# An SSM chunk scan on Trainium2: both channel groups kept on the partitions, signed phases in whole tiles on VectorE, output products of 64 rows

## The chip, the cores and the metric

The program runs on one core of a Trainium2 chip. A time is that of one execution on the device, in microseconds (us). The kernel before took 1131.76 us (median of three runs, 1124.91 to 1132.9). Where a profile is shown, it is one execution recorded by the hardware profiler. Engines are called PE (TensorE; PEld is its weight load), DVE (VectorE), ACT (ScalarE), POOL (GpSimd) and SP (SyncE, which here mostly issues DMAs).

## The reference, cut to what matters

A decoder trunk of two layers on 256 tokens, D = 1024, FF = 2816, all in fp32. Layer 0 has a SwiGLU FFN, differential attention, a second FFN and a gated embedding (ple); layer 1 the same with a diagonal state space model (SSM) and a gated linear unit (GLU) in place of attention. The change is in this SSM:

```python
def s5_glu(h, ...):          # 64 groups of 16 channels, 64 complex states each
    a_bar = jnp.exp(lam_dt); b_bar = ((a_bar - 1.0) / lam)[:, :, None] * b
    def chunk_step(state, u_c):                  # x[t] = a x[t-1] + b u[t], chunk by chunk
        bu = jnp.einsum('gph,bcgh->bcgp', b_bar, u_c.astype(jnp.complex64))
        _, xs = lax.associative_scan(combine, (a, bu), axis=1)
        xs = xs + a_pow[None] * state[:, None]
        y = jnp.einsum('ghp,bcgp->bcgh', c, xs).real + d_g * u_c
        return xs[:, -1], y
    ...
    z = jax.nn.gelu(y) @ w_glu + b_glu
    return z[..., :D_MODEL] * jax.nn.sigmoid(z[..., D_MODEL:])
```

## The kernel before, in words

**Threads and products.** The two blocks of 128 tokens (b = 0, 1) are two generators that share weight tiles, so their work alternates on every engine. Each large product is made of three fp32r products, hi x hi, lo x hi and hi x lo (`mm3`, L302 to L304). The order of instructions on each engine is fixed at build time by the Tile framework's scheduler, which plays the program through with its own estimates of durations and with priorities; on the chip each engine then runs its list strictly in that order.

**Weights** (`Weights`, L86 to L134) are streamed. SP issues a load of 512 KB into one of three `raw` buffers (L119), ACT casts it to `hi` (L131), VectorE makes `lo` = raw - hi (L133), and then the raw buffer is free for the next load. `hi` and `lo` come from pools of nine buffers each. The tiles of the GLU's weight `ssm_w_glu` have the numbers 252 to 267 (`raw252`, `hi252`, `lo252` and so on). Pairs of the same pools also take ready tables from DRAM (L111): for the SSM a `t_d` tile in `hi` and an `o_d` tile in `lo`.

**Tables** (`ssm_tables`, L754 to L965) are made while the FFN of layer 1 runs, about 330 to 680 us. They hold powers of a, the phases `er` and `ei` (cosine and sine of the rotation), the decay `rh`, and for each of 8 group packs (`gp`, eight groups) the complex products `vr`, `vi` and `or`, `oi` (`products`, L892 to L900, on POOL; `vr`/`vi` go through PE transposes `v_ps`, `or`/`oi` are stored to `o_d` by SP), and copies `cp` of C (L914, L915). POOL also computes the factors of the norms (`r_pre`, `r_pnple`, L313 to L317) for the layer's main work, between these. At the end POOL moves the Toeplitz blocks from `m_d` to `t_d` (L963).

**Scan stage** (`ssm_core`, L1005 to L1152, about 815 to 861 us). u is transposed to `ush`; `s_ps` = V u (chunks of 8 tokens) is copied to `ssmS` by ACT (L1076). Then, for each of four *pairs* `pr` (two group packs each, a tile 128x512 that holds real and imaginary part):
- PE transposes into `st_ps` (L1082), rows = 2 channel groups (e) x 64 states.
- VectorE rotates: t1 = st*er (L1101), t2 = swapped st*ei (L1110, L1111; for pairs 1 and 2 on POOL from a copy that ACT makes, L1104, L1106), w = t1 +- t2 (L1112 or L1107, L1108).
- two scans (L1114), one for the real and one for the imaginary part, turn w into y.
- it is rotated back: t1 = y*er (L1116 on VectorE), t2 on POOL (L1117, L1118).
- X, the state ahead of each chunk, is t1 +- t2 shifted by one, in four operations of 64 rows (L1125, L1126): the 64 rows of one e become two halves (real, imaginary) of a tile of 128 rows, in `ssmS` for even pairs, in `ush` for odd ones.
- PE accumulates `y_ps`: products(pr) = t_d * u (L1047) and outputs(pr) = o_d * X (L1058), each 16 products of 128 rows x 32 columns (each an instruction twice in the trace, since they are fp32). ACT applies gelu (L1065), one ACTIVATE of 128x512 for each pair.

The outputs of pair pr-1 are issued after X of pair pr. At the end the gelu's result is transposed (`y_tr`, L1146) and split into `yThi` (ACT, L325) and `yTlo` (VectorE, L326): half 0 comes from the pairs 0 and 1, half 1 from 2 and 3. The GLU (`zglu`, L302 to L304) begins with the products on half 0.

The line that turns a pair's products on its groups:

```python
nc.tensor.matmul(out_ap[32 * q:32 * q + 32], st_[:, 32 * q:32 * q + 32], w[:, q * P:(q + 1) * P], ...)   # grouped, q = 0..3
```

Of the kernel before, what the change touches and what calls it, by code (L numbers as in the profile page):

```python
# [9 lines left out]
F32 = mybir.dt.float32  # L10
F32R = mybir.dt.float32r
BF16 = mybir.dt.bfloat16
AF = mybir.ActivationFunctionType
ALU = mybir.AluOpType
AX = mybir.AxisListType

P = 128
# [23 lines left out]
 'pt2': [1, 2],  # L41
# [10 lines left out]
 'wait2': {},  # L52
 'xpr': [[1, 2, 3], []]}
# [89 lines left out]
def trunk(ctx, tc, x, p, norm_g, ffn_w_in, ffn_w_out, attn_w_qkv, attn_w_o, attn_lam, attn_subln_g,  # L143
          rel_bias, ssm_lam_re, ssm_lam_im, ssm_log_dt, ssm_b_re, ssm_b_im, ssm_c_re, ssm_c_im, ssm_d, ssm_w_glu,
          ssm_b_glu, ple_w_proj, ple_w_gate, out):
    nc = tc.nc
# [547 lines left out]
    ssm = {}  # L694
# [59 lines left out]
    def ssm_tables(pool, keep):  # L754
# [51 lines left out]
        ei = keep.tile([P, 8, 4, 32], F32, tag="ei", name="ei", bufs=1)  # L806
# [8 lines left out]
        ssm["er"], ssm["ei"], ssm["rh"] = er, ei, rh  # L815
# [12 lines left out]

# [37 lines left out]
        for nm, src in (("re", ssm_c_re), ("im", ssm_c_im)):  # L866
            ct = pool.tile([P, 4, 8, 16], F32, tag=f"c{nm}", name=f"c{nm}", bufs=1)
            csrc = src[0].rearrange("(a g) h p -> (g h) a p", g=8)
            for hf in range(2):
                cn = pool.tile([P, 4, 2, 64], F32, tag="cn", name=f"cn{nm}{hf}", bufs=1)  # L870
                for d_ in range(2):
                    nc.sync.dma_start(cn[:, :, d_, :], csrc[:, 4 * hf:4 * hf + 4, :])
                pt = bank("a1", f"c_ps{nm}{hf}")
                for a in range(4):
                    nc.tensor.transpose(pt[:, a * P:(a + 1) * P], cn[:, a].rearrange("p d n -> p (d n)"), ident)
                pv = pt.rearrange("p (q g e h) -> p q g e h", q=2, g=8, e=2)
                for e in range(2):
# [14 lines left out]
        def products(out_r, out_i, ar_, ai_, br_, bi_, nm):  # L892
# [4 lines left out]
            g.tensor_tensor(out_r, out_r, t, ALU.subtract)  # L897
# [8 lines left out]
        for gp in range(8):  # L906
# [34 lines left out]
            products(o_r, o_i, *A, *C, f"o{gp}")  # L941
# [58 lines left out]
    def take2(n):  # L1000
        W.advance(min(used[1] + NB, n + NB), n)
        used[0] = used[1] = n
        return W.tiles[n]

    def ssm_core(pool, vs, tos):  # L1005
# [28 lines left out]
        xfs = [[t[:, 2048 + 256 * e:2304 + 256 * e].rearrange("p (c j) -> p c j", j=32) for e in range(2)]  # L1034
               for t in (S_xf, ush_xf)]
# [5 lines left out]
        def grouped(out_ap, st_, w, **flags):  # L1041

            for q in range(4):
                nc.tensor.matmul(out_ap[32 * q:32 * q + 32], st_[:, 32 * q:32 * q + 32], w[:, q * P:(q + 1) * P],
                                 skip_group_check=True, **flags)

        def products(pr):  # L1047
            acc = ps_acc.tile([P, 512], F32, tag="acc", name=f"y_ps{pr}")
            nc.tensor.matmul(acc, zeros[:, :P], zeros, start=True, stop=False, skip_group_check=True)
            for gg in range(2):  # L1050
                tt, to = take2(tos[2 * pr + gg])
                for e in range(2):
                    j = 2 * gg + e
                    grouped(acc[:, j * P:(j + 1) * P], ush[:, 4 * pr + j, :], tt[:, e * 512:e * 512 + 512],
                            start=False, stop=False)
            return acc

        def outputs(pr, acc):  # L1058
            for gg in range(2):
                tt, to = W.tiles[tos[2 * pr + gg]]  # L1060
                for e in range(2):
                    j = 2 * gg + e
                    grouped(acc[:, j * P:(j + 1) * P], X[pr][e][:, gg * P:(gg + 1) * P], to[:, e * 512:e * 512 + 512],
                            start=False, stop=True)
            nc.scalar.activation(yg[:, pr // 2, :, 4 * (pr % 2):4 * (pr % 2) + 4, :].rearrange("p t g h -> p g t h"),  # L1065
                                 acc.rearrange("p (g t h) -> p g t h", g=4, t=8), AF.Gelu_apprx_tanh)

        for pr in range(4):
# [15 lines left out]
            er, ei, rh = (ssm[k][:, 2 * pr:2 * pr + 2].rearrange("p g q j -> p (g q j)") for k in ("er", "ei", "rh"))  # L1084
            er2 = er.rearrange("p (o x) -> p o x", o=1).broadcast_to([P, 2, 256])

            if pr % 2:
                r4 = big_pool.tile([P, 5, 2, 256], F32, tag="hT_lo1", name=f"rt{pr}")
                r4 = [r4[:, j] for j in range(5)]
            else:  # L1090
                r4 = [act_pool.tile([P, 2, 2, 256], F32, tag=f"xT_{x}{pr // 2}", name=f"rt{x}{pr}") for x in ("hi", "lo")]
                r4 = [t[:, j] for t in r4 for j in range(2)]

            def rt(nm):
                if nm == "s" and pr % 2 == 0:
                    return work.tile([P, 2, 256], F32, tag="sg", name=f"rts{pr}")
                return r4["abcds".index(nm)]
# [233 lines left out]
```

## Time and profile before

| | before |
|---|---|
| runs | 1131.76, 1124.91, 1132.9 us |
| profiled execution, its own time | 1130.13 us |
| its span (first to last instruction) | 1128.3 us |
| mean granted clock of PE | 0.971 |
| busy: PE, DVE, ACT, POOL | 1044.2, 694.4, 553.4, 258.9 us |
| moved by DMA | 218.62 MB |

The span is cut by time: what stands at 830 us of it happens in the scan stage. A row of a timeline has a start and a duration (a group of like instructions is put together in one row), then engine, line, operation, what it writes and what it reads; in brackets how long the engine had idled and who ended that. The granted clock is given as a part of full speed: 1.00 is 2.4 GHz, 0.50 is 1.2 GHz.

### The profile page before, as it was taken

The page shows a single profiled execution, that of the slowest core. Times are in us where ns is not written, and L with a number is a line of the kernel's source. Part 1 is how long each engine was busy: PE and PEld are TensorE (multiplying, and loading weights), DVE is VectorE, ACT ScalarE, POOL GpSimd, SP SyncE. Part 2 cuts the span into 40 slices and gives each one's busy share as a digit, 9 for nine tenths or more (in the row PEclk, how much of TensorE's full clock was granted, in tenths as well). Part 3 has the DMA queues.
Part 4 walks back from the last instruction along what each step waited for, and adds up shares of the span by engine and source line. Part 5 has one row for each costly group of instructions (what it writes and reads, how often), then busy time and mean ns, then how long its engine had stood idle before and what let it go on. Part 6 is the DMA issues. An engine that isn't in the chain of part 4 may idle for free. (4 is left out here: it accounts for less than half of the span.)

```text
span 1128.3 us, 14341 instructions
## 1 busy us (share of the span) xinstructions
PE 1044.2 (93%) x5123; PEld 836.1 (74%) x5123; DVE 694.4 (62%) x1011; ACT 553.4 (49%) x873; POOL 258.9 (23%) x315
## 2 busy tenths in 40 slices
PE   6899999999998999999787997999867999999997
PEld 4688888788776887777565886888645878888885
DVE  6555554679658896545568572654368675555464
ACT  5544443566665544443464542544244465444354
POOL 6000000000021007898879521000131010000001
PEclk9899999999999999999899998999987999999999
DMA  7766656567547767676555768756784557665651
GB/s 225 229 175 190 194 175 203 169 188 220 158 94 181 215 196 211 187 221 218 170 169 165 195 207 314 237 178 210 207 350 151 178 175 223 188 187 165 209 168 56
DMA packets 119815, 218.62 MB, mean 194 GB/s; under 512 B 25024, under 2 KB 43488, under 8 KB 119744
## 3 DMA queue, kind: packets, MB, share of 16 engines
q1 hardware_dynamic: 116864, 211.71, 61.3%
q0 software_dynamic: 1824, 5.33, 1.8%
q8 instruction: 40, 0.66, 0.2%
q10 hardware_dynamic: 1056, 0.66, 0.2%
q14 instruction: 31, 0.25, 0.1%
HBM read 205.13 MB, written 16.74 MB: 197 GB/s over the span
## 5 line engine op out<-in xcount | busy, mean ns | idle before, releaser
L133 DVE TENSOR_TENSOR lo<-raw,hi 128x1024 fp32r<-128x1024 f32 x332 | 427.5, 1294 | 271.1 <-ACT hi L131 269.4
L131 ACT CAST hi<-raw 128x1024 fp32r<-128x1024 f32 x332 | 347.6, 1051 | 334.7 <-PE up L304 105.5
L302 PE MATMUL up<-hi,xThi 128*128 128x512 f32 x704 | 279.6, 400 | 14.1 <-ACT hi L131 5.6
L304 PE MATMUL up<-hi,xTlo 128*128 128x512 f32 x704 | 280.3, 403 | 0.1
L303 PE MATMUL up<-lo,xThi 128*128 128x512 f32 x704 | 278.8, 397 | 1.6 <-DVE lo L133 1.6
L302 PEld LDWEIGHTS up<-hi,xThi 128*128 128x128 f32 x704 | 134.4, 191 | 43.5 <-ACT hi L131 6.4
L303 PEld LDWEIGHTS up<-lo,xThi 128*128 128x128 f32 x704 | 134.2, 191 | 31.5 <-DVE lo L133 3.9
L304 PEld LDWEIGHTS up<-hi,xTlo 128*128 128x128 f32 x704 | 134.0, 191 | 29.3 <-issue 0.6
L302 PE MATMUL dn<-hi,hThi 128*128 128x512 f32 x352 | 138.6, 395 | 0.0
L303 PE MATMUL dn<-lo,hThi 128*128 128x512 f32 x352 | 137.8, 391 | 0.0
L304 PE MATMUL dn<-hi,hTlo 128*128 128x512 f32 x352 | 137.7, 392 | 0.0
L313 POOL TENSOR_SCALAR v_pn<-sspn,sspn 128x1 f32<-128x1 f32 x8 | 3.4, 424 | 344.1 <-ACT junkpn L370 342.1
L304 PEld LDWEIGHTS dn<-hi,hTlo 128*128 128x128 f32 x352 | 66.4, 189 | 14.2 <-issue 0.2
L302 PEld LDWEIGHTS dn<-hi,hThi 128*128 128x128 f32 x352 | 66.4, 189 | 14.0 <-issue 0.6
L303 PEld LDWEIGHTS dn<-lo,hThi 128*128 128x128 f32 x352 | 66.4, 189 | 13.4
L321 ACT ACTIVATE xThi<-xT_ps,gT 128x128 fp32r<-128x128 f32 x112 | 38.7, 367 | 50.3 <-PE xT_ps L339 50.0
L326 DVE TENSOR_TENSOR hTlo<-hT_ps,hThi 128x512 fp32r<-128x512 f32 (+1 forms) x48 | 30.8, 644 | 39.8 <-ACT hThi L325 39.7
L325 ACT CAST hThi<-hT_ps 128x512 fp32r<-128x512 f32 (+1 forms) x48 | 26.4, 550 | 57.8 <-PE hT_ps L449 57.7
L322 DVE SCALAR_TENSOR_TENSOR xTlo<-xT_ps,gT,xThi 128x128 fp32r<-128x128 f32 x112 | 36.6, 345 | 21.8 <-ACT xThi L321 21.4
L339 PE MATMUL xT_ps<-ident,x 128*128 128x128 f32 x112 | 30.7, 300 | 16.4 <-DVE xTlo L322 11.0
L446 DVE SCALAR_TENSOR_TENSOR h<-up,r_pre,sg 128x512 f32<-128x512 f32 (+1 forms) x48 | 33.7, 703 | 13.1 <-ACT sg L444 7.8
L302 PE MATMUL qkvat<-hi,xThi 128*128 128x512 f32 x96 | 38.1, 397 | 0.2 <-ACT xThi L321 0.2
(358 smaller groups left out, 1303.9 us busy)
## 6 DMA issues: line engine op xcount, KB each, us to landing
raw<-in_ffn_w_in_dram SPq DMA_DIRECT2D x160, 512.0 KB, 4.3
raw<-in_ffn_w_out_dram SPq DMA_DIRECT2D x88, 512.0 KB, 4.1
raw<-in_attn_w_qkv_dram SPq DMA_DIRECT2D x24, 512.0 KB, 4.4
raw<-in_ffn_w_in_dram SPq DMA_DIRECT2D x32, 256.0 KB, 3.5
raw<-in_ple_w_gate_dram SPq DMA_DIRECT2D x16, 512.0 KB, 4.1
raw<-in_ssm_w_glu_dram SPq DMA_DIRECT2D x16, 512.0 KB, 4.4
gain<-in_norm_g_dram SPq DMA_DIRECT2D x8, 512.0 KB, 4.7
raw<-in_attn_w_o_dram SPq DMA_DIRECT2D x8, 512.0 KB, 4.0
```

The lines of the kernel that those rows point to most:

```text
L131: nc.scalar.copy(hi, raw)
L133: (nc.gpsimd if n in self.on_pool else nc.vector).tensor_tensor(lo, raw, hi.bitcast(F32), ALU.subtract)
L302: nc.tensor.matmul(out_ap, st_hi, w_hi, start=start, stop=False)
L303: nc.tensor.matmul(out_ap, st_hi, w_lo, start=False, stop=False)
L304: nc.tensor.matmul(out_ap, st_lo, w_hi, start=False, stop=stop)
L313: nc.gpsimd.tensor_scalar(v, parts[0], parts[1], eps, ALU.add, ALU.add)
L321: return (nc.scalar.activation(hi, psum, AF.Copy, scale=scale).ins, nc.vector.scalar_tensor_tensor(lo, psum, scale, hi.bitcast(F32), ALU.m ...
L322: nc.vector.scalar_tensor_tensor(lo, psum, scale, hi.bitcast(F32), ALU.mult, ALU.subtract).ins)
L325: nc.scalar.copy(hi, psum)
L326: nc.vector.tensor_tensor(lo, psum, hi.bitcast(F32), ALU.subtract)
L339: marks[b].append(nc.tensor.transpose(pt, xb[:, k * P:(k + 1) * P], ident).ins)
L446: nc.vector.scalar_tensor_tensor(h[:, :w], up_, r, sg[:, :w], ALU.mult, ALU.mult)
```

## The change

`eis` holds the phase twice, as [-ei, ei]. So the rotation works on whole tiles of 128x512: t1 = st*er, t2 = st with real and imaginary part swapped (`stv[:, ::-1]`) times eis, w = t1 - t2, and after the scans t1, t2 and X = t1 + t2, one shifted operation of 128x16x31. All six are on VectorE (`pt2` is empty); POOL and ACT have no part in it any more. X keeps e on its partitions: rows 0 to 63 are group e = 0, rows 64 to 127 e = 1, the real and the imaginary part lie side by side. An output product then has 64 rows: 2 packs x 2 parts x 2 e x 4 q = 32 for each pair in place of 16. They are accumulated in two banks for each half, `y_ps00`, `y_ps01` (half 0; e = 0, 1) and `y_ps10`, `y_ps11` (half 1), and gelu comes once for each bank after the odd pair. In the tables, c_im is negated where it leaves PSUM, `cp` of it is a plain copy, the order of `oi`'s products changes, and `o_d` is stored with 2 DMAs of 128 rows for each pack in place of 4 of 64. The ring for POOL's DMA descriptors (`dynamic_dma_scratch_size`) is set to 8192.

```diff
- 'pt2': [1, 2],
+ 'pt2': [],
...
-        ei = keep.tile([P, 8, 4, 32], F32, tag="ei", name="ei", bufs=1)
+        eis = keep.tile([P, 2, 8, 4, 32], F32, tag="ei", name="eis", bufs=1)
+        ei = eis[:, 1]
...
+        nc.gpsimd.tensor_scalar(eis[:, 0].rearrange("p g q j -> p (g q j)"), ei.rearrange("p g q j -> p (g q j)"), -1.0, None,
+                                ALU.mult)
...
-            g.tensor_tensor(out_i, ai_, br_, ALU.mult)
-            g.tensor_tensor(t, ar_, bi_, ALU.mult)
-            g.tensor_tensor(out_i, out_i, t, ALU.add)
+            g.tensor_tensor(out_i, ar_, bi_, ALU.mult)
+            g.tensor_tensor(t, ai_, br_, ALU.mult)
+            g.tensor_tensor(out_i, out_i, t, ALU.subtract if conj else ALU.add)
...
-                nc.gpsimd.tensor_scalar(cps[1][sl, :, e, :], c_im[sl, :, gp, :], -1.0, None, ALU.mult)
+                nc.gpsimd.tensor_copy(cps[1][sl, :, e, :], c_in[sl, :, gp, :])
...
-            for e in range(2):
-                for ri, t in enumerate((o_r, o_i)):
-                    nc.sync.dma_start(o_d[gp, ri * 64:ri * 64 + 64, e, :],
-                                        t[64 * e:64 * e + 64].rearrange("p q t h -> p (q t h)"))
+            for ri, t in enumerate((o_r, o_i)):
+                nc.sync.dma_start(o_d[gp, :, ri, :], t.rearrange("p q t h -> p (q t h)"))
...
-                for e in range(2):
-                    j = 2 * gg + e
-                    grouped(acc[:, j * P:(j + 1) * P], X[pr][e][:, gg * P:(gg + 1) * P], to[:, e * 512:e * 512 + 512],
-                            start=False, stop=True)
-            nc.scalar.activation(yg[:, pr // 2, :, 4 * (pr % 2):4 * (pr % 2) + 4, :].rearrange("p t g h -> p g t h"),
-                                 acc.rearrange("p (g t h) -> p g t h", g=4, t=8), AF.Gelu_apprx_tanh)
+                for r in range(2):
+                    for e in range(2):
+                        sl = slice(64 * e, 64 * e + 64)
+                        grouped(accs_y[hf][e][:, c0:c0 + P], X[pr][sl, r, gg * P:(gg + 1) * P], to[sl, r * 512:r * 512 + 512],
+                                start=False, stop=r == 1)
+            if pr % 2:
+                for e in range(2):
+                    nc.scalar.activation(yg[:, hf].rearrange("p t (x e) h -> p e t x h", e=2)[:, e],
+                                         accs_y[hf][e].rearrange("p (x t h) -> p t x h", x=4, t=8), AF.Gelu_apprx_tanh)
...
             v.tensor_tensor(t1, stv, er2, ALU.mult)
...
+            v.tensor_tensor(t2, stv[:, ::-1], eis, ALU.mult)
+            v.tensor_tensor(w, t1, t2, ALU.subtract)
             for ri in range(2):
                 v.tensor_tensor_scan(y[:, ri], rh, w[:, ri], 0.0, ALU.mult, ALU.add)
-            t1, t2 = rt("a"), rt("b")
             v.tensor_tensor(t1, y, er2, ALU.mult)
-            nc.gpsimd.tensor_tensor(t2[:, 0], y[:, 1], ei, ALU.mult)
-            nc.gpsimd.tensor_tensor(t2[:, 1], y[:, 0], ei, ALU.mult)
+            (nc.gpsimd if pr in OPT["pt2"] else v).tensor_tensor(t2, y[:, ::-1], eis, ALU.mult)
...
+            xl = v.tensor_tensor(xf[:, :, :, 1:32], t1v[:, :, :, 0:31], t2v[:, :, :, 0:31], ALU.add)
...
-    nc = _bacc.Bacc("TRN2", target_bir_lowering=False, num_devices=1)
+    nc = _bacc.Bacc("TRN2", target_bir_lowering=False, num_devices=1, dynamic_dma_scratch_size=8192)
```

The scheduler's order moves with it. ACT's list of the kernel before, from the gelu of pair 0 (`y_ps0`) on, ahead of the GLU; `hi255` is the cast of the fourth GLU weight tile:

```order
L1065 ACTIVATE ssmY_7137<-y_ps0_7182 128x4x8x16
L1065 ACTIVATE ssmY_7137<-y_ps1_7274 128x4x8x16
L1065 ACTIVATE ssmY_7137<-y_ps2_7370 128x4x8x16
L325 CAST yThi0_7505<-y_tr00_7509 128x4x16x4
L325 CAST yThi0_7505<-y_tr01_7518 128x4x16x4
L131 CAST hi255_7382<-raw255_7380 128x1024
L325 CAST yThi1_7507<-y_tr00_7509 128x4x16x4
L325 CAST yThi1_7507<-y_tr01_7518 128x4x16x4
L1065 ACTIVATE ssmY_7137<-y_ps3_7458 128x4x8x16
L131 CAST hi256_7388<-raw256_7386 128x1024
```

ACT's list of the changed kernel at the same place (`y_ps00`, `y_ps01` are half 0, `y_ps10`, `y_ps11` half 1):

```order
L1078 ACTIVATE ssmY_7122<-y_ps00_7161 128x32x16
L1078 ACTIVATE ssmY_7122<-y_ps01_7162 128x32x16
L130 CAST hi255_7378<-raw255_7376 128x1024
L130 CAST hi256_7384<-raw256_7382 128x1024
L130 CAST hi257_7474<-raw257_7472 128x1024
L130 CAST hi258_7480<-raw258_7478 128x1024
L130 CAST hi259_7573<-raw259_7571 128x1024
L130 CAST hi260_7617<-raw260_7615 128x1024
L1078 ACTIVATE ssmY_7122<-y_ps10_7364 128x32x16
L1078 ACTIVATE ssmY_7122<-y_ps11_7365 128x32x16
L324 CAST yThi0_7526<-y_tr00_7530 128x4x16x4
L324 CAST yThi0_7526<-y_tr01_7539 128x4x16x4
```

All six casts hi255 to hi260 now stand ahead of the gelu of half 1, and the first yThi behind it. On VectorE, the changed kernel from X of pair 2 (`ssmS` from `rthi2`) on:

```order
L1118 TENSOR_TENSOR ssmS_7121<-rthi2_7319 128x16x31
L1113 TENSOR_TENSOR rthi3_7421<-rtlo3_7422,er_3292 128x512
L1114 TENSOR_TENSOR rthi3_7421<-rtlo3_7422,eis_3293 128x512
L1118 TENSOR_TENSOR ush_7083<-rthi3_7421 128x16x31
L132 TENSOR_TENSOR lo255_7379<-raw255_7376,hi255_7378 128x1024
L132 TENSOR_TENSOR lo256_7385<-raw256_7382,hi256_7384 128x1024
L132 TENSOR_TENSOR lo257_7475<-raw257_7472,hi257_7474 128x1024
L132 TENSOR_TENSOR lo258_7481<-raw258_7478,hi258_7480 128x1024
L132 TENSOR_TENSOR lo259_7574<-raw259_7571,hi259_7573 128x1024
L132 TENSOR_TENSOR lo260_7618<-raw260_7615,hi260_7617 128x1024
L325 TENSOR_TENSOR yTlo0_7527<-y_tr00_7530,yThi0_7526 128x4x16x4
```

Before, only lo255 stood among the yTlo of half 0; the splits from lo256 on came behind them and between those of half 1. The splits lo252 and lo253 stand behind X of pair 1 and lo254 behind t2 of pair 2 now; before, all three stood behind two of the four operations of X of pair 1. On PE the changed kernel has, from the first output product of pair 2 on:

```order
L1048 MATMUL y_ps10_7364<-lo248_7060,ssmS_7121 32x128 x4
L1048 MATMUL y_ps11_7365<-lo248_7060,ssmS_7121 32x128 x4
L1048 MATMUL y_ps10_7364<-lo248_7060,ssmS_7121 32x128 x4
L1048 MATMUL y_ps11_7365<-lo248_7060,ssmS_7121 32x128 x4
L1048 MATMUL y_ps10_7364<-lo249_7166,ssmS_7121 32x128 x4
L1048 MATMUL y_ps11_7365<-lo249_7166,ssmS_7121 32x128 x4
L1048 MATMUL y_ps10_7364<-lo249_7166,ssmS_7121 32x128 x4
L1048 MATMUL y_ps11_7365<-lo249_7166,ssmS_7121 32x128 x4
L1048 MATMUL y_ps10_7364<-hi250_7177,ush_7083 32x128 x4
```

where before there were two rows of eight for the pair. products(3) (`hi250`, `hi251`) stands behind outputs(2) now, where it stood ahead of outputs(1) and between its products; the transposes `y_tr` of half 0 come behind outputs(3), and the first 20 products of the GLU ahead of those of half 1.

## Rows read from the trace of the kernel before

**Rows 1.** Page, part 1: busy time, share of the span, number of instructions.
```profile
PE 1044.2 (93%) x5123; PEld 836.1 (74%) x5123; DVE 694.4 (62%) x1011; ACT 553.4 (49%) x873; POOL 258.9 (23%) x315
```

**Rows 2.** Stretches: length, busy of PE, PEld, DVE, ACT, POOL; clock, DMA share, GB/s.
```profile
845.00:850.00 5.00, 1.50 (x24) 0.98 (x24) 4.94 (x5) 0.00 (x0) 2.10 (x3) 0.50 0.10 35
850.00:855.00 5.00, 3.45 (x59) 2.71 (x60) 4.83 (x10) 0.79 (x2) 1.10 (x3) 0.55 0.82 283
860.00:865.00 5.00, 5.00 (x33) 3.84 (x34) 4.39 (x7) 3.12 (x5) 0.00 (x0) 0.52 0.32 104
```

**Rows 3.** PE's waits, 862 to 1128: releaser, us in total, times, longest.
```profile
PE xT_ps L339 <- DVE x L377: 0.9, 1, 0.9
```

**Rows 4.** PE's waits, 830 to 862.
```profile
PE y_ps L1044 <- POOL ush L1125: 9.8, 2, 6.4
PE y_ps L1044 <- DVE ush L1125: 2.9, 1, 2.9
```

**Rows 5.** Timeline of VectorE, scan stage: start, us, engine, line, operation, tiles.
```profile
830.01 0.69 DVE L1101 TENSOR_TENSOR rthi<-st_ps,er 128x512 f32<-128x512 f32 x1 [1.61 <-PE st_ps L1082]
830.62 0.41 DVE L1110 TENSOR_TENSOR rthi<-st_ps,ei 128x256 f32<-128x256 f32 x1
...
832.12 1.27 DVE L1114 TENSOR_TENSOR_SCAN rtlo<-rh,rtlo 128x256 f32<-128x256 f32 x2
...
840.94 1.04 DVE L1116 TENSOR_TENSOR rt<-rt,er 128x512 f32<-128x512 f32 x1
...
846.56 3.89 DVE L133 TENSOR_TENSOR lo<-raw,hi 128x1024 fp32r<-128x1024 f32 x3
...
859.43 0.41 DVE L1125 TENSOR_TENSOR ush<-rt 64x248 f32<-64x248 f32 x1
```

**Rows 6.** Timeline of PE, scan stage: products, outputs and the first GLU product.
```profile
830.38 0.27 PE L1044 MATMUL y_ps<-hi,ush 128*32 128x128 f32 x1
...
839.70 1.08 PE L1044 MATMUL y_ps<-hi,ush 128*32 128x128 f32 x32
...
852.83 1.89 PE L1044 MATMUL y_ps<-lo,ssmS 128*32 128x128 f32 x32
...
861.34 0.80 PE L302 MATMUL zglu<-hi,yThi 128*128 128x512 f32 x1
```

**Rows 7.** Timeline of ACT at the end of the scan stage.
```profile
855.41 0.75 ACT L325 CAST yThi<-y_tr 128x256 fp32r<-128x256 f32 x2
...
861.47 0.60 ACT L1065 ACTIVATE ssmY<-y_ps 128x512 f32<-128x512 f32 x1 [0.43 <-PE y_ps L1044]
861.97 1.98 ACT L131 CAST hi<-raw 128x1024 fp32r<-128x1024 f32 x2
```

**Rows 8.** Timelines of VectorE and SP; landing of raw tiles, 840 to 900.
```profile
860.55 1.22 DVE L133 TENSOR_TENSOR lo<-raw,hi 128x1024 fp32r<-128x1024 f32 x1
...
861.79 0.37 SPq L119 DMA_DIRECT2D raw<-in_ssm_w_glu_dram  x1
...
DMA to landing us min/median/max: 3.6/4.0/5.5
```

**Rows 9.** PE's wait in the tables (440 to 640); timeline of POOL there and later.
```profile
PE v_ps L921 <- POOL vi L900: 8.9, 4, 3.4
...
423.67 0.18 POOL L903 MEMSET zt<- 16x112 f32 x1 [52.44 <-DVE cmb L709]
...
589.39 1.55 POOL L317 TENSOR_TENSOR r_pnple<-v_pnple,neg_half 128x1 f32<-128x1 f32 x1
...
593.48 1.88 POOL L914 COPY cp<-cre 64x64 f32<-64x64 f32 x2
595.43 1.27 POOL L900 TENSOR_TENSOR vi<-vi,ptv 128x512 f32<-128x512 f32 x1
...
673.66 6.04 POOL L963 DMA_DIRECT2D t_d<-m_d  x8 [3.17 <-DMA m_d<-msb]
...
798.31 0.36 POOL L978 MEMSET ssm_sel<- 128x128 f32 x2 [118.11 <-PE dn L304]
```

More of the change, by code (lines that the diff above doesn't have):

```diff
@@ L51 @@
  'wait': 3,
- 'wait2': {},
- 'xpr': [[1, 2, 3], []]}
+ 'wait2': {}}
 LAG = 5
@@ L814, in ssm_tables @@
         nc.gpsimd.tensor_copy(rh[:, :, :, 1:32], r8.rearrange(perm, q=4).broadcast_to([P, 8, 4, 31]))
-        ssm["er"], ssm["ei"], ssm["rh"] = er, ei, rh
+        ssm["er"], ssm["eis"], ssm["rh"] = er, eis, rh
         yield
@@ L877, in ssm_tables @@
                 for e in range(2):
-                    v.tensor_copy(ct[64 * e:64 * e + 64, 2 * hf:2 * hf + 2], pv[64 * e:64 * e + 64, :, :, e, :])
+                    dst, src_ = ct[64 * e:64 * e + 64, 2 * hf:2 * hf + 2], pv[64 * e:64 * e + 64, :, :, e, :]
+                    if nm == "re":
+                        v.tensor_copy(dst, src_)
+                    else:
+                        v.tensor_scalar(dst, src_, -1.0, None, ALU.mult)
             cs.append(ct)
             yield
-        c_re, c_im = cs
+        c_re, c_in = cs
         msb = pool.tile([P, 8, 2, 4, 16], F32, tag="msb", name="msb", bufs=1)
@@ L890, in ssm_tables, with products @@
         shp = [P, 4, 8, 16]
-        def products(out_r, out_i, ar_, ai_, br_, bi_, nm):
+        def products(out_r, out_i, ar_, ai_, br_, bi_, nm, conj=False):
             g = nc.gpsimd
@@ L940, in ssm_tables @@
             C = [t[:, :, gp:gp + 1, :].broadcast_to(shp) for t in cs]
[L941 to L945 removed]
+            products(o_r, o_i, *A, *C, f"o{gp}", conj=True)
+            for ri, t in enumerate((o_r, o_i)):
+                nc.sync.dma_start(o_d[gp, :, ri, :], t.rearrange("p q t h -> p (q t h)"))
             yield
@@ L1033, in ssm_core @@
         S = S_xf[:, :2048].rearrange("p (g r e n) -> p g r e n", g=8, r=2, e=2)
-        xfs = [[t[:, 2048 + 256 * e:2304 + 256 * e].rearrange("p (c j) -> p c j", j=32) for e in range(2)]
-               for t in (S_xf, ush_xf)]
+        xfs = [t[:, 2048:2560].rearrange("p (r c j) -> p r c j", r=2, j=32) for t in (S_xf, ush_xf)]
         yg = big_pool.tile([P, 2, 8, 8, 16], F32, tag="hT_hi0", name="ssmY")
@@ L1045, in grouped @@
                                  skip_group_check=True, **flags)
+        accs_y = {}
         def products(pr):
-            acc = ps_acc.tile([P, 512], F32, tag="acc", name=f"y_ps{pr}")
-            nc.tensor.matmul(acc, zeros[:, :P], zeros, start=True, stop=False, skip_group_check=True)
+            hf = pr // 2
+            if pr % 2 == 0:
+                accs_y[hf] = [ps_acc.tile([P, 512], F32, tag="acc", name=f"y_ps{hf}{e}") for e in range(2)]
+                for acc in accs_y[hf]:
+                    nc.tensor.matmul(acc, zeros[:, :P], zeros, start=True, stop=False, skip_group_check=True)
@@ L1050, in products @@
             for gg in range(2):
                 tt, to = take2(tos[2 * pr + gg])
+                c0 = (2 * (pr % 2) + gg) * P
                 for e in range(2):
-                    j = 2 * gg + e
-                    grouped(acc[:, j * P:(j + 1) * P], ush[:, 4 * pr + j, :], tt[:, e * 512:e * 512 + 512],
+                    grouped(accs_y[hf][e][:, c0:c0 + P], ush[:, 4 * pr + 2 * gg + e, :], tt[:, e * 512:e * 512 + 512],
                             start=False, stop=False)
-            return acc
@@ L1083, in ssm_core @@
                                         S[:, 2 * pr + gg, ri].rearrange("p e n -> p (e n)"), ident)
-            er, ei, rh = (ssm[k][:, 2 * pr:2 * pr + 2].rearrange("p g q j -> p (g q j)") for k in ("er", "ei", "rh"))
+            er, rh = (ssm[k][:, 2 * pr:2 * pr + 2].rearrange("p g q j -> p (g q j)") for k in ("er", "rh"))
             er2 = er.rearrange("p (o x) -> p o x", o=1).broadcast_to([P, 2, 256])
-            if pr % 2:
-                r4 = big_pool.tile([P, 5, 2, 256], F32, tag="hT_lo1", name=f"rt{pr}")
-                r4 = [r4[:, j] for j in range(5)]
-            else:
-                r4 = [act_pool.tile([P, 2, 2, 256], F32, tag=f"xT_{x}{pr // 2}", name=f"rt{x}{pr}") for x in ("hi", "lo")]
-                r4 = [t[:, j] for t in r4 for j in range(2)]
@@ L1094, in rt @@
[L1094 to L1097, printed above, removed]
+            eis = ssm["eis"][:, :, 2 * pr:2 * pr + 2].rearrange("p r g q j -> p r (g q j)")
+            if pr == 1:
+                r4 = big_pool.tile([P, 4, 2, 256], F32, tag="hT_lo1", name=f"rt{pr}")
+                t1, t2, w, y = (r4[:, j] for j in range(4))
+            else:
+                r4 = [act_pool.tile([P, 2, 2, 256], F32, tag=f"xT_{x}{pr // 2 % 2 if pr < 3 else 0}", name=f"rt{x}{pr}")
+                      for x in ("hi", "lo")]
+                t1, t2, w, y = (t[:, j] for t in r4 for j in range(2))
@@ L1134, in ssm_core @@
             if pr:
-                outputs(pr - 1, acc_y)
-            acc_y = products(pr)
+                outputs(pr - 1)
+            products(pr)
             if pr == OPT["sl"]:
                 W.hold = nullcontext, nullcontext
-        outputs(3, acc_y)
+        outputs(3)
         yT = [(act_pool.tile([P, KT, P], F32R, tag=f"xT_hi{b}", name=f"yThi{b}"),
```

31 lines of the change are left out of this document (7 added, 24 removed).

## The prediction

> **What bounds the kernel now.** I read the page's busy shares first: TensorE (PE) works 93% of the span [rows 1]. So I looked next for the places where PE waits, and for the stage that the change edits, by the table of stretches. PE is full from 860 on [rows 2], and from 862 to the end its longest wait is 0.9 us [rows 3]: from the first product of the GLU at 861.34 [rows 6] the engine has work without a break up to the end of the span. Whatever the change gains or loses before that product moves the end by as much, so **the start of the GLU is the quantity to forecast**.
>
> Ahead of it lies the scan stage, 830 to 861. There PE waits 12.7 us for `ush`, the tile in which X of the pairs 1 and 3 lies [rows 4]. But the engine behind those waits is mostly VectorE: it is busy 4.94 of 5 us in 845 to 850 and 4.83 of 5 in 850 to 855 [rows 2], POOL only 2.10 and 1.10. The reader should see a queue of VectorE work from 830.01 to 859.84, where X of pair 3 is finished [rows 5], then outputs(3) on PE, then the GLU at 861.34 [rows 6]. In this stage PE's clock is at its lower level for much of the time (0.50 in 845 to 850, 0.55 in 850 to 855, 0.52 in 860 to 865) [rows 2].
>
> **The change, part by part.**
>
> *Rotation and X on VectorE.* Per pair there are now six passes of 128x512 (t1, t2 and w before the scans, t1, t2 and X after them) and two scans; POOL and ACT take no part. Price of a pass: 0.61 us from start to start when the next one does not need it (830.01 to 830.62, in [rows 5]), 0.69 alone. Two scans: 1.27 [rows 5], in a queue about 1.2. The row of 1.04 is the same pass while POOL works beside it [rows 5]; POOL is now idle, so I take 0.61 and keep 1.04 as the upper bound for the four plus four passes that read with the two halves swapped, a pattern for which no row exists. In the order of the changed kernel 24 passes, 4 pairs of scans and the three splits lo252 to lo254 stand from t1 of pair 0 to X of pair 3: 24 x 0.61 + 4 x 1.2 + 3.89 [rows 5] = 23.3 us. From 830.0 this gives X of pair 3 at about 853.3, against 859.84: 6.5 us earlier. Split up in the same way, X of pair 1 is done at 844.1 (17 passes, 3 pairs of scans) and X of pair 2 at 851.4. With the upper bound, 8 x 0.43 = 3.4 us later.
>
> *Output products of 64 rows.* outputs(p) has 32 products where it had 16; each product is two instructions in the trace, so 64 in place of 32. No row shows a tile of 64 rows. Lower bound: the products of the two row halves run beside each other, as those of the four column groups do now (32 instructions in 1.08 us, though a single one lasts 0.27) [rows 6]; then a pair costs what it does now, 1.08 at the full clock and 1.89 at the lower [rows 6]. Upper bound for work in sequence: twice that, 3.8 at the lower clock. After X of pair 2 (851.4) PE has outputs(2), products(3) (1.89, as many instructions as a pair of outputs before) and outputs(3) left: the end lies at 851.4 + 1.9 + 2 x 1.9 = 857.1, or 851.4 + 1.9 + 2 x 3.8 = 860.9. I take the lower one, since the column groups of the rows do overlap; it will turn out that the difference decides little.
> The Trainium skill, "TensorEngine Tiling (Array Packing)", Key Properties, says that tiles operate independently and can run in parallel; by that the sum takes 857.1. No run so far shows it for row halves.
>
> *Gelu by halves, and what ACT does before it.* Here is the term that I think decides. Before, ACT had the gelu of pair 2, the first yThi, and only then the casts hi255 on. Now, in ACT's order, the six casts hi255 to hi260 stand between the gelu of half 0 and that of half 1, and the first yThi, which the first GLU product needs, stands behind both. A cast needs its raw tile; there are three raw buffers, and one comes free when its lo split is done: before, lo255 runs 860.55 to 861.77 and the next raw load is issued at 861.79 [rows 8]. In the new order of VectorE lo255 to lo260 stand behind X of pair 3. So:
> - lo255 853.3 to 854.5, lo256 to 855.7, lo257 to 857.0 (1.22 each) [rows 8];
> - the raw tile of hi260 is issued at 857.0 and lands 4.0 us later (3.6 to 5.5) [rows 8]: 861.0;
> - hi260 ends at 861.1 + 1.05 = 862.2 (two casts take 1.98) [rows 7];
> - two gelus of 0.60 [rows 7]: 863.4; two yThi in 0.75 [rows 7]: 864.1; the first GLU product at about 864.3.
>
> That is 864.3 - 861.34 = **3.0 us later**. outputs(3) at 857.1, or even at 860.9, is ready before hi260, so the saving of 6.5 us on VectorE ends as idle time of PE, waiting for ACT. What is late next: nothing, since g0 to g8 (the pairs 252 to 260) are all split by then. The first eight GLU products ran at the lower clock before (0.52) [rows 2], after a wait of PE; they will again, so this term is zero.
>
> *The tables* (POOL's work, 440 to 640). PE waits there 8.9 us for `vi` in four places, the longest 3.4 [rows 9]. Sixteen POOL operations of the cp copies become plain copies; the two that stand before the last operation of `vi` for one group (1.88 us, 593.48 to 595.43) [rows 9] now stand behind it, so that wait can shrink by 1.9. Against that the changed order of the products puts one product (1.27) [rows 9] ahead of r_pnple (1.55) [rows 9], for which VectorE's x update waits. The negation of eis (one POOL pass of 128x1024) falls in an idle time of 52 us [rows 9] and costs nothing; without that cover it would cost some 2.5 us, twice the 1.27 of a pass half as long [rows 9]. The o_d stores are 16 DMAs in place of 32 on SP's queue, at 0.37 us of issue each, going by a weight load [rows 8]: SP gets 6 us back that nothing waited for. I take -1 us for the tables, between -2 and +2.
>
> *Half the descriptor ring.* If it makes POOL wait in t_d<-m_d, it delays rows that last 6.04 us and behind which POOL idles 118 us [rows 9]; t_d is first loaded after 798. Cost zero; if the cover were gone, at most a second pass of 6 us.
>
> **Sum**: 1130.13 (the profiled execution, span 1128.3 and 1.83 around it) + 3.0 - 1 = 1132.1. The median of the runs shown is 1131.76, so the forecast is: no change that can be measured. About 1%, 11 us, is what a measurement of this kernel can tell from none.
>
> **Rivals.**
> - *The casts do not hold the gelu up.* If the raw tiles land early enough, half 1 follows outputs(3): 857.1 + 1.2 + 0.75 + 0.2 = 859.3 with overlap, or 863.0 without, which is -2.0 or +1.7, and with the table term 1127 to 1131. For it: PE is done by then. Against it: hi260 must end before 857.1, so X of pair 3 would have to be done 5 us before 853.3, and VectorE's sum has no such slack.
> - *Row halves in sequence, with a pause at each switch* (the slower side). The place is outputs(2) and outputs(3), 128 instructions. One alone lasts 0.27 [rows 6]; with no overlap at all the two would take 35 us, the GLU would start at 851.4 + 1.9 + 35 + 2.1 = 890, and the time would be 1158. It decides from the point where outputs(2) and outputs(3) take more than 9 us (71 ns an instruction), and is slower by 1% from 17 us on (136 ns). Against it: the column groups overlap in every row.
>  The Trainium skill, same page and section, says that changing the tiling mode drains the engine. By it each change between products(p) and outputs(p) would cost a drain, some ten in the stage; no row here shows one.
> - *Swapped halves at 1.04 a pass*: +3.4 on X of pair 3 and on the whole chain behind it: 1135.5.
> - *The tables fall the other way.* A new order of PE and POOL over 200 us can move more than I can follow in rows: four waits for `vi` of 8.9 us in all could go (about 1125), or be joined by as much (1140).
>
> **How the numbers follow.** The ACT chain as forecast 0.50 (1129 to 1135); casts not in the way 0.17 (1127 to 1131); swapped passes dear 0.11 (1135 to 1137); tables better by more than 3 us 0.08, worse by more than 3 us 0.07; row halves in sequence 0.07 (1136 up). From 1125 to 1138 all but some 0.2 are held, with the spread of the execution beside it. Faster by over 1% needs nearly the whole of the waits for `vi` besides the casts rival: 0.05. Slower by over 1% is half of the row-halves rival and a part of the tables: 0.07. The rest, 0.88, is no change.
>
> **What would show it.** In the profile after: VectorE's last X ends near 853; POOL is idle in the stage; ACT shows a wait ahead of hi259 or hi260 that ends with a raw load, and the gelus of half 1 directly behind hi260; PE's wait before the first yT or GLU product is put down to ACT and lasts 4 to 7 us; the GLU starts near 864. Wrong would be: an outputs group of more than 4 us, passes near 1.0 us, gelus of half 1 that wait for PE, or a table stage (440 to 640) whose PE time differs by more than 3 us.

## The result, and the profile after

The changed kernel took 1140.89 us (median of 7, 1137.45 to 1144.62) against 1131.76 (median of 7, 1124.91 to 1134.55): ratio 1.0087, 95% interval 1.0064 to 1.0109. It is slower by 9 us; 1132.1, within 1125 to 1138, had been forecast, so the result lies outside the range. The profiled execution took 1143.69 us, with a span of 1141.9. Lines in the changed kernel are one less than before at the helpers (L132 for the lo split, L301 to L303 for the three products) and five to seven more in the tables.

First the page, part 1 (as [rows 1]), of the changed kernel:

```profile
PE 1055.5 (92%) x5251; PEld 844.4 (74%) x5251; DVE 686.9 (60%) x1004; ACT 551.6 (48%) x871; POOL 241.7 (21%) x297
```

VectorE and POOL have less to do, as intended; PE is busy 11 us longer though only 128 small instructions were added. Busy time of PE also grows when its clock is low (before, the 32 instructions of a pair took 1.08 us at a clock of 1.00 and 1.89 at 0.54 [rows 6]), so this alone names no cause. The question is in which stage the time was lost, and three marks answer it: the first rotation on VectorE (start of the scan stage), the first GLU product, and the end of the span.

| profiled execution | first rotation | first GLU product | scan stage | from there to the end |
|---|---|---|---|---|
| before | 830.01 | 861.34 | 31.3 | 267.0 |
| changed | 839.28 | 874.25 | 35.0 | 267.7 |
| difference | +9.3 | +12.9 | +3.6 | +0.7 |

So there are two losses: 3.6 us in the scan stage and 9.3 ahead of it, where the tables are made.

**The scan stage.** Timeline of VectorE in the changed kernel (columns as in [rows 5]):

```profile
839.28 0.69 DVE L1108 TENSOR_TENSOR rthi<-st_ps,er 128x512 f32<-128x512 f32 x1 [1.99 <-PE st_ps L1095]
839.89 0.68 DVE L1109 TENSOR_TENSOR rthi<-st_ps,eis 128x512 f32<-128x512 f32 x1
...
861.79 0.68 DVE L1118 TENSOR_TENSOR ush<-rthi 128x496 f32<-128x496 f32 x1
862.38 3.49 DVE L132 TENSOR_TENSOR lo<-raw,hi 128x1024 fp32r<-128x1024 f32 x3
```

From the first pass to the end of the last X it is 862.47 - 839.28 = 23.2 us, where [rows 5] had 29.8. The pass with swapped halves (0.68, and 0.6 to the next start) costs no more than a plain one. Timeline of PE in the same stage (as [rows 6]):

```profile
860.58 1.96 PE L1048 MATMUL y_ps<-lo,ssmS 64*32 64x128 f32 x64 [4.03 <-issue]
862.47 1.93 PE L1048 MATMUL y_ps<-hi,ush 128*32 128x128 f32 x32
864.34 1.27 PE L1048 MATMUL y_ps<-lo,ush 64*32 64x128 f32 x64
865.54 1.09 PE L1136 MATMUL y_tr<-ident,ssmY 128*128 128x128 f32 x8
...
874.25 0.79 PE L301 MATMUL zglu<-hi,yThi 128*128 128x512 f32 x1 [7.62 <-ACT yThi L324]
```

outputs(3) is done at 865.6; after the transposes PE waits 7.6 us for yThi. Timeline of ACT (as [rows 7]):

```profile
867.71 1.04 ACT L130 CAST hi<-raw 128x1024 fp32r<-128x1024 f32 x1 [3.88 <-DMA raw<-in_ssm_w_glu_dram]
870.38 1.04 ACT L130 CAST hi<-raw 128x1024 fp32r<-128x1024 f32 x1 [1.62 <-DMA raw<-in_ssm_w_glu_dram]
871.64 1.04 ACT L130 CAST hi<-raw 128x1024 fp32r<-128x1024 f32 x1 [0.22 <-DMA raw<-in_ssm_w_glu_dram]
872.59 1.07 ACT L1078 ACTIVATE ssmY<-y_ps 128x512 f32<-128x512 f32 x2
873.55 0.65 ACT L324 CAST yThi<-y_tr 128x256 fp32r<-128x256 f32 x2
```

The three casts hi258 to hi260 wait for raw loads, and the gelus of half 1, whose products had been complete since 865.6, stand behind them. The 6.6 us that VectorE won are spent here.

**The tables.** Timelines of POOL, SP and VectorE of the kernel before, in that order:

```profile
633.19 1.65 POOL L900 TENSOR_TENSOR oi<-oi,pto 128x512 f32<-128x512 f32 x1
634.79 5.32 POOL L960 DMA_DIRECT2D m_d<-msb  x7
640.60 0.50 POOL L953 DMA_DIRECT2D dg<-in_norm_g_dram  x1 [0.49 <-issue]
...
634.86 1.09 SPq L944 DMA_DIRECT2D o_d<-oi  x2
...
647.80 0.41 DVE L954 TENSOR_TENSOR db<-db,dg 16x256 f32<-16x256 f32 x1 [1.46 <-DMA dg<-in_norm_g_dram]
```

Those of POOL, SP, VectorE and PE of the changed kernel, 635 to 678 (`dg` and `db` are small tiles of the last table step; POOL issues their loads, VectorE multiplies them):

```profile
636.09 5.32 POOL L965 DMA_DIRECT2D m_d<-msb  x7
641.39 1.34 POOL L907 TENSOR_TENSOR oi<-oi,pto 128x512 f32<-128x512 f32 x1
653.60 0.50 POOL L958 DMA_DIRECT2D dg<-in_norm_g_dram  x1 [10.87 <-DMA o_d<-oi]
...
635.06 13.68 SPq L118 DMA_DIRECT2D raw<-in_ffn_w_in_dram  x6
648.83 0.42 SPq L950 DMA_DIRECT2D o_d<-oi  x1
...
657.22 0.41 DVE L959 TENSOR_TENSOR db<-db,dg 16x256 f32<-16x256 f32 x1 [4.92 <-DMA dg<-in_norm_g_dram]
...
675.45 0.41 DVE L959 TENSOR_TENSOR db<-db,dg 16x256 f32<-16x256 f32 x1 [1.01 <-DMA db<-in_ssm_d_dram]
...
677.26 0.73 DVE L445 SCALAR_TENSOR_TENSOR h<-up,r_pre,sg 128x512 f32<-128x512 f32 x1
...
678.04 1.12 PE L448 MATMUL hT_ps<-ident,h 128*128 128x128 f32 x4 [3.33 <-DVE h L445]
```

POOL's list now has the seven m_d stores (5.3 us of issue) ahead of the last operation of `oi`; before, they stood behind it. So `oi` is ready at 642.7. Its store stands in SP's list behind raw loads that wait for buffers, and leaves at 648.8, where it left at 634.9 before. The tile `dg` takes the buffer of `oi`, so its load waits 10.9 us for that store; VectorE waits 4.9 us for `dg` (1.5 before) with the lo splits behind it, and the later `db` operations, late as well, stand ahead of an `h` for which PE waits 3.3.

From the last v_ps transpose to the last `up` product of this FFN it is 758.5 - 630.2 = 128.3 us in the changed kernel and 749.5 - 625.3 = 124.2 before. The rest of the 9.3 lies ahead, and part of it need not be the change's. Stretches of the kernel before, then of the changed one (as [rows 2]), around two waits of PE for `vi` that are about as long in both (1.6 to 1.7 us):

```profile
462.00:472.00 10.00, 8.60 (x49) 6.99 (x50) 3.37 (x4) 4.24 (x7) 5.87 (x8) 1.00 0.53 178
510.00:522.00 12.00, 10.29 (x56) 7.96 (x55) 6.32 (x4) 4.88 (x7) 8.85 (x10) 1.00 0.67 218
```

```profile
462.00:472.00 10.00, 8.29 (x42) 6.31 (x40) 3.04 (x3) 3.27 (x5) 4.14 (x7) 0.83 0.45 152
510.00:522.00 12.00, 10.40 (x52) 7.46 (x52) 7.04 (x4) 3.60 (x5) 7.42 (x8) 0.86 0.51 159
```

In this execution of the changed kernel the clock fell after both waits, and the lag behind the kernel before grew from 0.9 us (463.40 against 464.30, the end of the first of the two) to 4.0 (537.36 against 541.34, the end of the next such wait behind them). This happens in kernels of either order: of the nine profiled executions of this document, the clock was below 1.00 in the first stretch in two (0.83 in the changed kernel and in mdscan) and in the second in three (0.86 in the changed kernel, in od4scan and in the ring experiment, the last two with the table order of the kernel before). The profiled execution is 2.8 us above its median; that these falls are the reason is not shown.

### The profile page after: what moved, and what is told of

It reads as the page before. It is cut to its first block, busy times and chain, and to the rows that moved or that the text cites. A ratio compares the mean times of both kernels' runs of the same rounds, so it can differ in the third digit from the quotient of the medians.

```text
span 1141.9 us, 14521 instructions
## 1 busy us (share of the span) xinstructions
PE 1055.5 (92%) x5251; PEld 844.4 (74%) x5251; DVE 686.9 (60%) x1004; ACT 551.6 (48%) x871; POOL 241.7 (21%) x297
## 5 line engine op out<-in xcount | busy, mean ns | idle before, releaser
L132 DVE TENSOR_TENSOR lo<-raw,hi 128x1024 fp32r<-128x1024 f32 x332 | 425.9, 1289 | 275.8 <-ACT hi L130 273.6
L301 PE MATMUL up<-hi,xThi 128*128 128x512 f32 x704 | 281.6, 403 | 13.1 <-ACT xThi L320 7.1
L303 PE MATMUL up<-hi,xTlo 128*128 128x512 f32 x704 | 281.5, 405 | 0.1
L301 PEld LDWEIGHTS up<-hi,xThi 128*128 128x128 f32 x704 | 135.3, 192 | 43.0 <-ACT xThi L320 9.7
L302 PEld LDWEIGHTS up<-lo,xThi 128*128 128x128 f32 x704 | 135.4, 192 | 31.4 <-DVE lo L132 3.5
L303 PEld LDWEIGHTS up<-hi,xTlo 128*128 128x128 f32 x704 | 134.9, 193 | 29.6 <-issue 0.6
L301 PE MATMUL dn<-hi,hThi 128*128 128x512 f32 x352 | 139.5, 397 | 0.0
L303 PE MATMUL dn<-hi,hTlo 128*128 128x512 f32 x352 | 138.3, 394 | 0.0
L301 PEld LDWEIGHTS dn<-hi,hThi 128*128 128x128 f32 x352 | 66.8, 190 | 14.3 <-issue 0.8
L303 PEld LDWEIGHTS dn<-hi,hTlo 128*128 128x128 f32 x352 | 66.8, 190 | 14.2
L301 PE MATMUL qkvat<-hi,xThi 128*128 128x512 f32 x96 | 38.1, 397 | 0.2 <-ACT xThi L320 0.2
```

What stands on the lines that cost most here:

```text
L132: (nc.gpsimd if n in self.on_pool else nc.vector).tensor_tensor(lo, raw, hi.bitcast(F32), ALU.subtract)
L301: nc.tensor.matmul(out_ap, st_hi, w_hi, start=start, stop=False)
L302: nc.tensor.matmul(out_ap, st_hi, w_lo, start=False, stop=False)
L303: nc.tensor.matmul(out_ap, st_lo, w_hi, start=False, stop=stop)
```

## The experiments

Ratios are to the kernel before, run beside each on the same chip. "Table stretch" is the time from the last v_ps transpose to the last `up` product in the profiled execution, as above. Two things are asked: is the table loss due to the order or to the work, and is the scan loss due to the casts ahead of the gelu?

| kernel | ratio, 95% interval | table stretch, us | scan stage, us |
|---|---|---|---|
| before | 1 | 124.2 | 31.3 |
| changed | 1.0087 (1.0064 to 1.0109) | 128.3 | 35.0 |
| four o_d stores again (od4) | 1.0032 (1.0010 to 1.0054) | 122.8 | 34.9 |
| m_d behind oi (md) | 1.0031 (1.0013 to 1.0049) | 125.5 | 34.9 |
| dg in its own buffer (dg) | 1.0036 (1.0019 to 1.0052) | 120.8 | 35.1 |
| three casts behind yThi (scan) | 0.9999 (0.9982 to 1.0017) | 126.2 | 28.7 |
| od4 and scan (od4scan) | 0.9959 (0.9944 to 0.9973) | 121.9 | 27.9 |
| md and scan (mdscan) | 0.9970 (0.9951 to 0.9988) | 120.4 | 28.0 |
| before, with the halved ring | 1.0002 (0.9989 to 1.0015) | 121.7 | 31.4 |

**Four stores again.** Of all parts of the change, splitting the store of `o_d` again is enough to bring the table stage back to the order of the kernel before.

```diff
-                nc.sync.dma_start(o_d[gp, :, ri, :], t.rearrange("p q t h -> p (q t h)"))
+                for e in range(2):
+                    nc.sync.dma_start(o_d[gp, 64 * e:64 * e + 64, ri, :], t[64 * e:64 * e + 64].rearrange("p q t h -> p (q t h)"))
```

> The changed kernel with one thing undone: the o_d tables are stored with four DMAs of 64 rows for each pack again, in the new layout; the computation is the same. The scheduler then puts the table stage in the order of the kernel before (SP's list has no difference to it at all). Theory A (the table stage lost its time through the new order that the fewer stores brought: in the trace of the changed kernel the last store of oi leaves at 648.8 in place of 634.9, the dg loads wait for it, and VectorE stands behind them): the first GLU product comes about 5 us earlier than in the changed kernel, ratio to the kernel before 1.002 to 1.006 (about 1136). Theory B (the loss comes from the work itself, such as the negated phases, the copies or the halved descriptor ring): ratio stays at 1.0087 (about 1141).

Measured: 1.0032. Timelines of this kernel, POOL, then VectorE's first rotation and PE's first GLU product:

```profile
631.49 1.66 POOL L907 TENSOR_TENSOR oi<-oi,pto 128x512 f32<-128x512 f32 x1
633.10 5.31 POOL L966 DMA_DIRECT2D m_d<-msb  x7
638.81 0.50 POOL L959 DMA_DIRECT2D dg<-in_norm_g_dram  x1 [0.39 <-issue]
...
826.04 0.69 DVE L1109 TENSOR_TENSOR rthi<-st_ps,er 128x512 f32<-128x512 f32 x1 [1.62 <-PE st_ps L1096]
...
860.94 0.79 PE L301 MATMUL zglu<-hi,yThi 128*128 128x512 f32 x1 [6.82 <-ACT yThi L324]
```

`oi` is again ahead of m_d, the wait ahead of `dg` is gone, and 0.0055 of the 0.0087 (6 us, with some 3 us of uncertainty) with it; the scan stage is as long as in the changed kernel, and the 3.6 us that are left are what that stage had lost. The work of the tables (signed phases, copies, the other order of the products) was in both, so it is not what cost the time: theory A.

**The casts behind yThi.** The loads of the tiles 258 to 260 are issued in the program after the split of y, and their cast and split are queued behind the first two yThi and yTlo; the tables keep the changed order.

```diff
+            if pr == 2:
+                W.limit = g0 + 6
             products(pr)
...
-                    split_plain(pv[:, b], *dst)
+                    sp = split_plain(pv[:, b], *dst)
+                    if (hf, tt, b) == (0, 1, 0):
+                        yc, yl = sp
         ssm["yT"] = yT
+        W.limit = len(specs)
+        W.gate = g0 + 6, g0 + 9, lambda: tc.issue_after(yc.ins), lambda: tc.issue_after(yl.ins)
```

> The changed kernel with one thing added: the casts and splits of the GLU tiles 258 to 260 are queued behind the first two yThi and yTlo, so that the gelu of half 1 does not stand behind them on ACT; the table stage is in the order of the changed kernel. Theory A (casts that wait for raw loads hold the gelu): the GLU starts some 1.5 to 2.5 us after the end of outputs(3), 28 to 29 us after the first rotation in place of 35.0, and the time falls by 6 us: ratio to the kernel before about 1.003 (1.000 to 1.005). Theory B (outputs of 64 rows or VectorE bound the end of the stage): under 1 us falls, ratio 1.008.

Measured: 0.9999, 0.0088 less than the changed kernel (10 us, where 6 were expected, and just below the expected 1.000 to 1.005). Timeline of ACT, then the first GLU products on PE, then PE's stretch at the start of the GLU:

```profile
859.27 1.08 ACT L1081 ACTIVATE ssmY<-y_ps 128x512 f32<-128x512 f32 x2 [2.09 <-PE y_ps L1050]
860.24 0.66 ACT L326 CAST yThi<-y_tr 128x256 fp32r<-128x256 f32 x2
860.76 1.08 ACT L132 CAST hi<-raw 128x1024 fp32r<-128x1024 f32 x1
...
860.95 0.50 PE L303 MATMUL zglu<-hi,yThi 128*128 128x512 f32 x1 [0.72 <-ACT yThi L326]
861.29 0.39 PE L304 MATMUL zglu<-lo,yThi 128*128 128x512 f32 x1
...
860.00:865.00 5.00, 4.28 (x21) 3.34 (x19) 3.39 (x5) 4.10 (x7) 0.00 (x0) 1.00 0.65 226
```

The gelus now wait for PE, as they should, and the GLU follows them: 28.7 us from the first rotation (832.27) to the GLU, 6.3 less. Part of what lies beyond that has a visible cause: PE had waited 0.7 us only, and the clock was full from the first GLU product on, so that the part from there to the end took 265.8 us instead of 267.7. What is left of the 10 us lies within the intervals.

**Both.** The same two edits together.

> Both together: four o_d stores for each pack, and the casts 258 to 260 behind the first yThi. If the two losses are separate and add up: the changed kernel's time less 5 and less 6, about 1129 to 1131, ratio to the kernel before 0.997 (0.994 to 1.001), with a GLU start 28 to 29 us after the first rotation. If one of them only uncovers the other's wait: ratio 1.003 or more.

Measured: 0.9959, with the GLU 27.9 us after the rotation. The two losses are separate and add up within the intervals (0.0055 and 0.0088 one by one, 0.0128 together), and this version is faster than both kernels, by 4.6 us than the one before. VectorE's first rotation, then PE:

```profile
829.09 0.69 DVE L1112 TENSOR_TENSOR rthi<-st_ps,er 128x512 f32<-128x512 f32 x1 [1.73 <-PE st_ps L1099]
...
854.15 1.16 PE L1051 MATMUL y_ps<-lo,ush 64*32 64x128 f32 x64
...
856.97 0.50 PE L303 MATMUL zglu<-hi,yThi 128*128 128x512 f32 x1 [0.64 <-ACT yThi L326]
```

**The ring alone**, in the kernel before.

```diff
-    nc = _bacc.Bacc("TRN2", target_bir_lowering=False, num_devices=1)
+    nc = _bacc.Bacc("TRN2", target_bir_lowering=False, num_devices=1, dynamic_dma_scratch_size=8192)
```

> The kernel before with the halved ring of DMA descriptors alone (8192); the order of no engine changes. If the ring costs nothing on the path (POOL idles 118 us behind its last table DMA): ratio 1.000, within 0.998 to 1.002. If the halved ring is what made the table stage late: ratio 1.004 to 1.006.

Measured: 1.0002: nothing. POOL's timeline of this kernel shows what it does, where [rows 9] had eight t_d issues without a pause:

```profile
675.53 5.28 POOL L963 DMA_DIRECT2D t_d<-m_d  x7 [3.73 <-DMA m_d<-msb]
682.84 0.76 POOL L963 DMA_DIRECT2D t_d<-m_d  x1 [2.03 <-issue]
```

The eighth waits 2.0 us (1.9 to 3.2 in the eight kernels with this ring), in POOL's idle time. In this execution, too, the clock was 0.86 in 510 to 522 after a wait of PE as long as before, and the table order is that of the kernel before: such a fall is not the change's doing.

**Which link of the chain.** What is still open after od4 is whether the chain oi, store, dg, VectorE costs the 6 us, or another place at which the order moved (the second block's x update, 596 to 630). Two kernels keep the two stores and cut the chain at different links. In the first, m_d is queued behind `oi`:

```diff
-            products(o_r, o_i, *A, *C, f"o{gp}", conj=True)
+            oi_last = products(o_r, o_i, *A, *C, f"o{gp}", conj=True)
...
-            nc.gpsimd.dma_start(m_d[:, :, 7 + k, :], m16[16 * k:16 * k + 16])
+            with tc.issue_after(oi_last.ins):
+                nc.gpsimd.dma_start(m_d[:, :, 7 + k, :], m16[16 * k:16 * k + 16])
```

> The changed kernel, two stores for each pack, with one pair of POOL's list put back: the seven m_d stores stand behind the last operation of oi again, as in the kernel before; the rest of the table stage keeps the changed order (r_pnple and the second block's xThi too). Theory A1 (the loss is the chain: oi late, its store behind raw loads on SP, dg waits for the store because it takes oi's buffer, VectorE waits for dg with lo splits behind it): POOL's wait ahead of dg falls from 10.9 us to under 3, VectorE's wait ahead of the first db from 4.9 to under 2, and the ratio to the kernel before falls from 1.0087 to 1.003 to 1.005. Theory A2 (the loss lies before, in the second block's x update and xThi, 596 to 630): ratio 1.007 to 1.009.

Measured: 1.0031. POOL's and SP's timelines:

```profile
633.16 2.17 POOL L907 TENSOR_TENSOR oi<-oi,pto 128x512 f32<-128x512 f32 x1
635.28 5.35 POOL L966 DMA_DIRECT2D m_d<-msb  x7
640.70 0.50 POOL L958 DMA_DIRECT2D dg<-in_norm_g_dram  x1
...
635.36 0.34 SPq L950 DMA_DIRECT2D o_d<-oi  x1
```

With that one pair put back, the whole 6 us are back. POOL's list differs from the changed kernel's in this pair alone; in the lists of the other engines the store of `oi` moved ahead of raw loads again, and behind it VectorE's `db` operations and some of PE's products of the FFN (650 to 731) changed places too. In the second, `dg` has a buffer of its own:

```diff
-            dg = pool.tile([16, 16, 16], F32, tag="vi", name=f"dg{q}", bufs=1)
+            dg = pool.tile([16, 16, 16], F32, tag="dg", name=f"dg{q}", bufs=1)
```

> The changed kernel, two stores for each pack and the m_d stores ahead of oi as they are, but the dg tiles have a buffer of their own in place of oi's, so that no load of dg has to wait for the store of oi. Theory A1: though the store of oi leaves as late as before (about 640 to 650), VectorE does not wait for dg and the ratio falls to 1.003 to 1.005. Theory A1b (the late store hurts by its place on SP, not through dg) or A2 (the loss lies ahead of 630): ratio 1.007 to 1.009.

Measured: 1.0036. SP and VectorE:

```profile
641.17 0.42 SPq L950 DMA_DIRECT2D o_d<-oi  x1
...
645.27 0.41 DVE L959 TENSOR_TENSOR db<-db,dg 16x256 f32<-16x256 f32 x1
```

The store of `oi` still leaves 7 us after `oi` was begun (634.11), but nobody waits for it: VectorE takes its first `db` operation without idle time. So the late store hurts through `dg`. The free buffer also moved other operations on VectorE, ACT and PE, most of them between 637 and 731. That the three remedies, with three different orders behind them, end at the same ratio (1.0031 to 1.0036) speaks against these as the cause. The last link shows in PE's waits for `h` between 630 and 720: 3.9 us in the changed kernel and 2.4 in scan, the two in which `dg` waits for the store, and at most 0.5 in the other seven.

**m_d behind oi, and the casts behind yThi.**

> The m_d stores behind oi, and the casts 258 to 260 behind the first yThi. If A1 holds and the two losses add up, this is as fast as the version with four stores: ratio 0.996 (0.994 to 0.998), about 1125. If A2 holds: the same as with the casts moved alone, 1.000.

Measured: 0.9970, with the stage at 28.0 us: as expected, and as with four stores within the intervals.

## Why the prediction was wrong, point by point

- **PE is full from the GLU on, and what is lost ahead of it is lost at the end.** Right: behind the first GLU product the changed kernel's PE waits at most 1.4 us, and +12.9 at that product became +13.6 at the end.
- **VectorE's queue.** Right: 23.3 us were forecast up to the last X, 23.2 measured; the upper bound of 1.04 for swapped halves did not occur.
- **Outputs of 64 rows.** Right at the lower bound: 64 instructions in 1.96 us at the lower clock and 1.16 to 1.27 higher up (granted 0.50, then 0.91 to 1.00), against 1.89 and 1.08 for 32 of 128 rows. The Trainium skill's sentence that tiles operate independently ("TensorEngine Tiling (Array Packing)", Key Properties) agrees with these rows. The drain at a change of tiling mode that the Trainium skill names in the same section does not show as a gap: outputs(3) starts at 864.34, inside the 1.93 of the products that begin at 862.47.
- **The gelu behind the casts.** Right in place and sign: 3.0 us forecast, 3.6 measured, 3.6 to 3.8 in every kernel that kept this order. lo255 began 23.1 us after the first rotation (23.3 forecast). The mis-sized term is the landing of the last raw tile: 4.0 us were taken, and hi260 began 5.7 after the issue of its load (865.9, the second of the two issues from 864.76 on, to 871.64), just above the 3.6 to 5.5 of [rows 8]; what followed was 0.6 shorter. PE's wait was 7.6 us, where 4 to 7 had been named.
- **The GLU's first products at the lower clock.** Right for the changed kernel (0.67 in 875 to 880), but it is no constant: where PE does not wait long before them they run at the full clock (1.00 in 860 to 865 of scan), and from there to the end it took 265.8 us instead of 267.7.
- **The ring.** Right: nothing that can be measured.
- **What can be told from none.** "About 1%, 11 us" was too coarse: the interval of the ratio reaches 0.0022 (2.6 us) to each side, so the 9 us stand clear of none.
- **The tables: the step that failed.** "I take -1 us for the tables, between -2 and +2" was worth +6 by the changed kernel against its three remedies (0.0051 to 0.0056), and +3 to +5 where the casts are moved (0.9999 against 0.9970 and 0.9959), each with some 3 us of uncertainty; by the table stretch it is 4.8, the mean of the two kernels with the chain (127.3) less that of the other seven (122.5). It priced the operations that were removed and one product that moved, by their durations. The stores of o_d were taken as "SP gets 6 us back that nothing waited for": true of the queue time, but the scheduler reacts to it, and two of POOL's list entries changed places, with a store, a shared buffer and VectorE's queue behind them. POOL's list of the changed kernel shows m_d ahead of `oi`; it was not followed there: t_d had been judged by the 118 us of idle time behind it [rows 9], m_d had no term at all, and of POOL the rows between 597 and 673, where the chain lies, were not shown; the stage that was watched ended at 640. What waits is not m_d's reader but the operation queued behind m_d. The rival "the tables fall the other way" named 1140 us and had a chance of 0.07, but its mechanism, longer waits for `vi`, did not occur: PE waited 7.0 us for `vi` in 440 to 640 instead of 8.9, so that its number is near by luck. The other shifts of the table stage, which the forecast did weigh (`vi` earlier, the longest wait 2.1 instead of 3.4; r_pnple later), come to nothing that shows within 2 us: md has them and od4 has not, and their ratios are 1.0031 and 1.0032.

With the two terms as measured, 3.6 and 3 to 6, the result of 9.1 is accounted for within the intervals.

## What to carry to other kernels

An edit that removes only cheap work can move the lists of all engines; for each issue that changes places, price what stands behind it in its own queue, and follow the buffers that it frees late, not only the reader of its data. A faster engine ahead of a join gains nothing if the join's other operands are queued, on an in-order engine, behind work that waits for DMA: look at what stands directly ahead of the last operation before the join. When a faster version comes out slower, first cut the time at marks that both kernels have; two separate losses, as here, may then each have a small remedy.

## What the runs showed of the hardware

- Products of 64 rows that alternate between the two row halves, each half into its own bank, cost in pairs within 10% what one product of 128 rows does (64 instructions in 1.96 us at a granted clock of 0.50 and 1.16 at 1.00, beside 32 in 1.89 at 0.54 and 1.08 at 1.00).
- A VectorE pass whose input has its two halves in reverse order takes 0.68 us, the plain one 0.69.
- With the halved ring, POOL's eighth DMA in a row waited 1.9 to 3.2 us; with the ring of the kernel before, eight went without a pause.
- After the same wait of 1.7 us PE's clock stayed full in some executions (1.00 in 510 to 522 of the kernel before) and fell in others (0.86 there in the ring experiment). In the changed kernel, with two such falls, the lag behind the kernel before grew by 3.1 us over that part; how much of it the falls cost is not shown.
